# Raw left operands on GpSimd's DMA queue, a shorter pace for the last keys, fewer copies of x, and a last product in two banks

## The chip, the cores and the metric

The kernel runs on one core of a Trainium2 chip. The core has engines that run side by side, each through its own instructions in order: TensorE (PE, with its weight loads shown apart as PEld), VectorE (DVE), ScalarE (ACT), GpSimd (POOL) and SyncE (SP). DMAs are issued from the queues of SP, ACT and POOL and then run on 16 DMA engines. The metric is the device time of one execution in microseconds (us); lower is better. Three runs of the kernel before took 2245.58, 2249.1 and 2252.1 us (median 2249.1).

## What is computed

One inference step of a one-layer streaming encoder with two groups of eight heads: stick-breaking attention and retention. 1024 prompt rows and 8 x 16 sample rows (decoding against a cache of 1024 frames) go through it, all in fp32. Shortened:

```python
h = rms_norm(x, norm_pre)
q_sb, k_sb, v_sb, gate_sb, q_r, k_r, v_r, gate_r = split(h @ w_in)      # rope on q_r, k_r
o_sb = stick_breaking(q_sb, k_all, v_all)      # k_all: cached keys, then the new ones
o_r, state = retention(q_r, k_r, v_r, state)   # chunks of 64
y = concat(head_rms(o_sb) * g_sb * silu(gate_sb), head_rms(o_r) * g_r * silu(gate_r))
out = y @ w_out
x = x + rms_norm(out, norm_post)
```

The new keys, values and states are outputs too.

## The kernel before

**Products.** Each fp32 operand is split into a high part (ACT, L173) and the rest (DVE, L174), and a product is three passes on PE: high x high, high x low, low x high. The helper `split` does this for weights (raw tile `wr`, parts `wh`, `wl`) and for left operands (raw `mr`, `yr` or `ys`; parts `mh`, `ml` or `ah`, `al`). In the profile its work has lines L173 and L174 whatever calls it, so tiles tell who.

**Two stages.** The first stage projects and runs attention, in two groups of rows (0: prompt tiles 0 to 3 and the sample; 1: prompt tiles 4 to 7) and by heads, with projections on PE at L405 and L462. The second stage is the output product as a one-level Strassen scheme: seven products of half-size blocks, in two 512-column halves each, with PE at L1218, L1221 and L1222 (`times`). Their left operands are blocks of `s_y` (written by the heads) or sums of blocks (`s_s`, made by the `sums` jobs from `br`, L303 to L330); their weights are `w_out` or sums of its blocks (`s_b`), loaded at L1235 on SP's queue, two blocks ahead, into five buffers.

**The order of the work.** Side work is written as generators, here called jobs. While the program is recorded, `tick` is called after every few matmuls and moves each due job by a step; a `yield n` says how many ticks until the next step. A tick lies one and a half matmuls (in the first products of the second stage) to three matmuls apart. So the numbers in `yield` and in the D_ constants set where in each engine's order the work of a job stands. What an engine or a queue then waits for is decided by semaphores at run time. `pin` only ties a step to its place in the order and adds no wait of its own.

**The left operands.** `left` (L333) loads two rows of blocks at a time (a pair: 128 x 2 x 256 fp32, 256 KB) into `deep` buffers (three for `mr`, two for `yr`), yields `wait` ticks, and then splits one of eight blocks every D_OP = 2 ticks; after each second split it issues the load of the next pair that has no buffer yet. `left_sample` (L355) does the same with the sample's rows. Both issue on SP's queue (L343, L361), the queue of the weight loads. `both` (L1376) makes these jobs for the later products, with `wait` = D_LEFT // 3 = 8 ticks; the products of the middle of the first stage use D_LEFT = 24 and aren't touched.

**POOL's queue.** POOL issues the stick-breaking attention's transfers through memory (`s_be`, `be`, L653 and L662), the cached keys, `gpost` (the gain of the last norm, L1316) and the stores of the output that add to what is there (L1358). It also masks (L687).

**Decoding.** `decode` (L809) runs for each head beside the projections: keys come in eight loads, one step of the job each D_ZC = 23 ticks; then scores, weights, and the values `vc`, eight loads of 512 KB on SP's queue (L863) into six buffers, used by matmuls at L897 in an order of k = 0 to 7. The loads of k = 6 and 7 need the buffers of k = 0 and 1.

**Residuals.** `residuals` (L378) copies x to the output, one DMA of 512 columns by 128 rows at a time on ACT's queue, 36 in all, one every 50 ticks; later stores add to it or write over it.

**The end.** The last product (1, 1) is done in two halves of 256 columns in one PSUM bank. DVE subtracts each half from the row (L1484), ACT squares it with a sum (L1485), and the norm's small steps (L1489 to L1496) join both sums with `known`, that of the row's other parts.

Of the kernel before, what the change touches and what calls it, by code (L numbers as in the profile page):

```python
# [14 lines left out]
ALU = mybir.AluOpType  # L15
# [3 lines left out]
P = 128  # L19
D = 2048  # L20
KT = D // P
H = 8
# [15 lines left out]
D_ZP = (2, 2)  # L38
D_Z0 = (19, 11)
D_AV = (9, 11)  # L40
D_ZC = 23
D_ROW = 18
D_VC = (6, 36)
V_BUFS = 6
# [17 lines left out]
D_LEFT = 24  # L62
D_SUM2 = (4, 6, 26)
D_SUM3 = (3, 3, 6)
MR = 3
AHEAD = 2
HT = KT // 2
# [24 lines left out]
def tile_hybrid_step(  # L92
# [105 lines left out]
    def pin(*made):  # L198
        if anchor[0] is not None:
            for ins in made:  # L200
                tc.add_manual_dep(
                    ins.ins,
                    anchor[0].ins.name,
                    mybir.DependencyInfo(mybir.DependencyClass.NoSync, mybir.DependencyReason.SCHED_ONLY),
                    reason="not ahead of the products",
                )
# [126 lines left out]
    def left(gi, n, hi, lo, bufs, tag, deep, wait):  # L333
        src = LEFT[n]
        raw = []

        def load(pair):
            r = bufs.tile([P, 2, 256], F32, name=tag, tag=tag, bufs=deep)
            if src[0] == "y":
                rows = s_y[gi][src[1] * H // 2 + pair][:, :, src[2] * 256 : src[2] * 256 + 256]  # L340
            else:
                rows = s_s[gi][pair][:, :, src[1], :]
            pin(nc.sync.dma_start(r, rows))  # L343
            raw.extend((r[:, 0], r[:, 1]))

        for pair in range(deep):
            load(pair)
        yield wait
        for h in range(HT):
            pin(*split(hi[h], lo[h], raw.pop(0)))  # L350
            if h % 2 and h // 2 + deep < HT // 2:
                load(h // 2 + deep)
            yield D_OP

    def left_sample(kk, hi, lo, bufs, tag, deep, wait):  # L355
        raw = []
        for part in range(2):
            r = bufs.tile([P, HT // 2, P], F32, name=tag, tag=tag, bufs=deep)
            for i in range(2):
                pair = (kk * H + part * HT // 2) // 2 + i  # L360
                pin(nc.sync.dma_start(r[:, 2 * i : 2 * i + 2], s_y[0][pair][:, :, 4 * P : 5 * P]))  # L361
            raw.extend(r[:, i] for i in range(HT // 2))
        yield wait
        for h in range(HT):
            pin(*split(hi[h], lo[h], raw.pop(0)))
            yield D_OP

    preset = {}

    def after_preset(ins, t, c):  # L370
        tc.add_manual_dep(
            ins.ins,
            preset[t, c].ins.name,
            mybir.DependencyInfo(mybir.DependencyClass.Sync, mybir.DependencyReason.DATA),
            reason="the rows hold their input",
        )

    def residuals():  # L378
        for t in range(NT):
            for c in range(4):  # L380
                cs = slice(c * 512, (c + 1) * 512)
                preset[t, c] = nc.scalar.dma_start(y_rows(t)[:, cs], x_rows(t)[:, cs])
                pin(preset[t, c])
                yield 50

    def operand(pool, tags, n, **kw):
        made = [pool.tile([P, HT, n], F32R, name=t, tag=t, **kw) for t in tags]
# [88 lines left out]
    with ExitStack() as s1:  # L476
# [332 lines left out]
        def decode(h, qs, rest):  # L809
# [18 lines left out]
            for m in range(NB + 1):  # L828
                if m > 0 and m % 4 == 0:
                    s, ks = m // 4 - 1, ready[:4]  # L830
                    del ready[:4]
                    z = score_tile("zc")
                    for j in range(2):
                        for c in range(4):
                            r = slice(32 * c, 32 * c + 32)
                            mm = nc.tensor.matmul(  # L836
                                z[r, :],
                                qp[:, j, r],
                                ks[2 * j + c // 2][0][:, c % 2, :],
                                start=(j == 0),  # L840
                                stop=(j == 1),
                            )
                            if j == c == 0:

                                tc.add_manual_dep(
                                    mm.ins,
                                    ks[3][1].ins.name,
                                    mybir.DependencyInfo(
                                        mybir.DependencyClass.NoSync, mybir.DependencyReason.SCHED_ONLY
                                    ),  # L850
                                    reason="a set at a time",
                                )
                    with tc.issue_after(mm.ins):
                        with_scores()
                    sigmoids(kp, be, s * 512, z)
                if m + KC_AHEAD < NB:
                    load_k(m + KC_AHEAD)
                if m < NB:
                    yield D_ZC

            def load_v(k):
                vc = ip.tile([P, NB, P], F32, name="vc", tag="kv", bufs=V_BUFS)
# [443 lines left out]
    with ExitStack() as s3:  # L1306
# [68 lines left out]
        def both(n, groups):  # L1375
            made = []  # L1376
            for g in groups:
                mine[g, n] = operand(c3, ("ah", "al"), 256, bufs=2) if g else kept(at[n])
                made.append(left(g, n, *mine[g, n], *((rp, "yr", 2) if g else (wp, "mr", MR)), D_LEFT // 3))
            return made  # L1380

        def jobs_of(made):
# [33 lines left out]
        (first,) = both(1, G1)  # L1416
        more = Job(sums(fp, [sum_rows(1, h) for h in range(EARLY, H)], D_SUM3, 3), 30)
        Job(load_gpost(), 40)
        ready = [Job(left_sample(1, *mine["s", 1], fp, "ys", 2, D_LEFT // 3), 24)]
        for p in range(4):  # L1420
            outs[1, p] = rp.tile([P, D], F32, name=f"out{p}", tag=f"out{p}")
        Job(collect(1, 1, product(1, 1, G0, True, 2, first)), 1)
# [35 lines left out]
        for g, p in LAST:  # L1458
            key = g, 2 + p
            if g == 0:  # L1460
                load_row((1, p))
            a = bank()
            final = (g, p) == LAST[-1]
            halves = [slice(i * 256, i * 256 + 256) for i in range(2)]
            for hs in halves if final else (slice(0, 512),):
                for k in range(HT):
                    blocks = (half[k][:, hs] for half in keep)
                    times(a[:, hs], mine[g, 4], k, TS[p], *blocks, k == 0, k == HT - 1, k == 0)
                    if (g, p) == (0, 0):
                        tick()  # L1470
                        tick()
            if (g, p) == (0, 0):
                while jobs:
                    tick()
            o = area(key, 1)
            ssq = ssqs[key][0]
            known = rp.tile([P, 1], F32, name="known", tag="known", bufs=2)
            nc.vector.tensor_tensor(known, ssq[:, 2:3], ssq[:, 3:4], ALU.add)
            nc.vector.tensor_tensor(known, known, ssq[:, 0:1], ALU.add)
            nc.vector.tensor_scalar(known, known, 1.0 / D, EPS, ALU.mult, ALU.add)  # L1480
            base = [rp.tile([P, 1], F32, name=f"base{i}", tag=f"base{i}", bufs=2) for i in range(2)]
            sq = rp.tile([P, 512], F32, name="sq3", tag="sq3", bufs=1)
            for hs, part in zip(halves, base):
                nc.vector.tensor_tensor(o[:, hs], o[:, hs], a[:, hs], ALU.subtract)  # L1484
                nc.scalar.activation(sq[:, hs], o[:, hs], AF.Square, accum_out=part)  # L1485
            t = scaled[g][:, p, :]
            nc.vector.tensor_tensor(t, o, gpost[:, 512:1024], ALU.mult)
            v, hv, r, u = (rp.tile([P, 1], F32, name=f"end{i}", tag=f"end{i}") for i in range(4))
            nc.vector.tensor_scalar(v, base[0], 1.0 / D, known, ALU.mult, ALU.add)  # L1489
            nc.vector.tensor_scalar(v, base[1], 1.0 / D, v, ALU.mult, ALU.add)  # L1490
            nc.scalar.activation(r, v, AF.Sqrt)
            nc.vector.tensor_scalar(hv, v, -0.5, None, ALU.mult)
            nc.vector.reciprocal(r, r)
            nc.vector.tensor_scalar(u, r, r, hv, ALU.mult, ALU.mult)
            rs = rp.tile([P, 1], F32, name="rs", tag="rs", bufs=2)
            nc.vector.scalar_tensor_tensor(rs, u, 1.5, r, ALU.add, ALU.mult)  # L1496
            for c in (0, 2, 3, 1):
                part = t if c == 1 else area(key, c)
                x = rows[g, p][:, c * 512 : (c + 1) * 512]
                if c or final:  # L1500
                    for i, hs in enumerate(halves if final and c == 1 else (slice(0, 512),)):
                        nc.vector.scalar_tensor_tensor(part[:, hs], part[:, hs], rs, x[:, hs], ALU.mult, ALU.add)
                        store(key, c, (nc.sync, nc.scalar)[final and (c == 2 or i)], part[:, hs], hs)
                else:
                    nc.scalar.activation(part, part, AF.Copy, scale=rs)
                    add_out(key, c)
# [108 lines left out]
```

## Time and profile before

| | |
|---|---|
| median of three runs | 2249.1 us |
| the profiled execution, its own time | 2247.99 us |
| its span on the core | 2246.0 us |
| mean granted clock of TensorE | 0.997 |
| moved by DMA | 471.24 MB |

The span is what the profiler saw on the core; the profiled execution's own time has 2.0 us more around it. In the views, a row of a timeline has start and duration in us, engine, line, operation, output <- input, shape, and how many instructions it joins; the bracket at its end is the idle time just before it and what ended that. "SPq" and "ACTq" are a DMA's issue on that queue. A row of the waits has the engine and line that waited, what released it, and the total, the number and the longest of these waits. A row of the chain has start, duration and what the chain went through. A row of the DMA list ends with the size of each transfer and the median us from issue to landing. A row of windows has the length, then busy time and instructions of PE, PEld, DVE, ACT and POOL, the granted clock (1.00 is full), the share of DMA engines busy and GB/s.

### The profile page before, as it was taken

The page shows a single profiled execution, that of the slowest core. Times are in us where ns is not written, and L with a number is a line of the kernel's source. Part 1 is how long each engine was busy: PE and PEld are TensorE (multiplying, and loading weights), DVE is VectorE, ACT ScalarE, POOL GpSimd, SP SyncE. Part 2 cuts the span into 40 slices and gives each one's busy share as a digit, 9 for nine tenths or more (in the row PEclk, how much of TensorE's full clock was granted, in tenths as well). Part 3 has the DMA queues.
Part 4 walks back from the last instruction along what each step waited for, and adds up shares of the span by engine and source line. Part 5 has one row for each costly group of instructions (what it writes and reads, how often), then busy time and mean ns, then how long its engine had stood idle before and what let it go on. Part 6 is the DMA issues. An engine that isn't in the chain of part 4 may idle for free.

```text
span 2246.0 us, 34685 instructions
## 1 busy us (share of the span) xinstructions
PE 2217.6 (99%) x12026; PEld 1887.3 (84%) x12026; DVE 1266.2 (56%) x2690; ACT 919.8 (41%) x1999; POOL 432.2 (19%) x723
## 2 busy tenths in 40 slices
PE   8999999999999999999999999999999999999998
PEld 7888889798888979888788888888888888878887
DVE  5335445453444545356666675656666757646667
ACT  6423333333333333334333343443434445545563
POOL 1022131222213132221222111120202213000020
PEclk9999999999999999999999999999999999999999
DMA  8567575576657557678768778978888787765786
GB/s 290 172 200 202 175 195 172 179 194 209 185 180 192 183 170 198 204 202 278 223 183 237 231 230 239 242 229 232 232 242 231 219 230 199 234 204 165 223 205 181
DMA packets 383105, 471.24 MB, mean 210 GB/s; under 512 B 120400, under 2 KB 237904, under 8 KB 382416
## 3 DMA queue, kind: packets, MB, share of 16 engines
q1 hardware_dynamic: 252688, 290.84, 43.8%
q0 software_dynamic: 36432, 95.72, 15.6%
q10 hardware_dynamic: 93808, 82.46, 11.7%
q8 instruction: 94, 1.54, 0.3%
q14 instruction: 83, 0.68, 0.1%
HBM read 367.97 MB, written 110.36 MB: 213 GB/s over the span
## 4 chain that ended last, share of the span: by engine, by line
PE 87%; DMA 5%; DVE 3%; issue 3%; ACT 2%; SPq 1%; POOL 0%; DVEq 0%; ACTq 0%; POOLq 0%
PE accm L462 34%; PE acc L405 29%; PE a L1221 5%; PE a L1218 5%; PE a L1222 5%; PE z L768 2%; PE pa L795 2%; PE zc L836 1%; PE pd L897 1%; DMA s_rk<-rk 1%; DMA ro<-s_rk 1%; DMA wr<-w_cols 1%; DMA vc<-cache_v 1%; PE rs L918 1%; PE pa L936 1%
## 5 line engine op out<-in xcount | busy, mean ns | idle before, releaser
L173 ACT ACTIVATE wh<-wr 128x512 fp32r<-128x512 f32 x408 | 256.9, 631 | 481.8 <-PE acc L405 200.5
L462 PE MATMUL accm<-whn,mh 128*128 128x512 f32 x1152 | 452.6, 393 | 0.5 <-DVE rk L508 0.5
L462 PE MATMUL accm<-whn,ml 128*128 128x512 f32 x1152 | 452.6, 393 | 0.0
L462 PE MATMUL accm<-wln,mh 128*128 128x512 f32 x1152 | 452.1, 392 | 0.0
L405 PE MATMUL acc<-mh,wh 128*128 128x256 f32 (+2 forms) x1536 | 444.2, 340 | 7.3 <-ACT wh L173 7.3
L405 PE MATMUL acc<-ml,wh 128*128 128x256 f32 (+2 forms) x1536 | 446.4, 341 | 0.0
L405 PE MATMUL acc<-mh,wl 128*128 128x256 f32 (+2 forms) x1536 | 444.4, 340 | 0.0
L174 DVE TENSOR_TENSOR wl<-wr,wh 128x512 fp32r<-128x512 f32 x408 | 279.4, 688 | 268.8 <-ACT wh L173 253.6
L174 DVE TENSOR_TENSOR wln<-wrn,whn 128x512 fp32r<-128x512 f32 x256 | 175.5, 689 | 278.3 <-ACT whn L173 270.0
L173 ACT ACTIVATE whn<-wrn 128x512 fp32r<-128x512 f32 x256 | 161.2, 632 | 388.8 <-PE accm L462 268.4
L405 PEld LDWEIGHTS acc<-mh,wh 128*128 128x128 f32 x1536 | 284.1, 189 | 26.3 <-ACT wh L173 7.3
L405 PEld LDWEIGHTS acc<-mh,wl 128*128 128x128 f32 x1536 | 282.1, 189 | 23.9 <-issue 5.3
L405 PEld LDWEIGHTS acc<-ml,wh 128*128 128x128 f32 x1536 | 281.4, 189 | 19.3 <-issue 1.2
L462 PEld LDWEIGHTS accm<-whn,mh 128*128 128x128 f32 x1152 | 216.7, 188 | 44.7 <-DVE rk L508 1.3
L462 PEld LDWEIGHTS accm<-whn,ml 128*128 128x128 f32 x1152 | 216.7, 188 | 43.3 <-issue 0.8
L462 PEld LDWEIGHTS accm<-wln,mh 128*128 128x128 f32 x1152 | 216.6, 188 | 42.9
L662 POOL DMA_DIRECT2D be<-s_be x128 | 93.9, 739 | 150.1 <-DMA s_be<-be 127.0
L698 DVE TENSOR_TENSOR_SCAN kp<-kp 128x1152 f32<-128x1152 f32 (+4 forms) x40 | 82.6, 2066 | 55.3 <-POOL kp L693 28.0
L1218 PE MATMUL a<-wh,mh 128*128 128x512 f32 x240 | 94.8, 395 | 0.9 <-ACT mh L1278 0.9
L1222 PE MATMUL a<-wh,ml 128*128 128x512 f32 x240 | 93.7, 391 | 0.0
L1221 PE MATMUL a<-wl,mh 128*128 128x512 f32 x240 | 93.7, 390 | 0.0
L1218 PE MATMUL a<-wh,ah 128*128 128x512 f32 x208 | 82.4, 396 | 2.9 <-ACT wh L173 2.9
(285 smaller groups left out, 2942.5 us busy)
## 6 DMA issues: line engine op xcount, KB each, us to landing
wr<-w_cols SPq DMA_DIRECT2D x256, 256.0 KB, 4.5
wrn<-w_rows SPq DMA_DIRECT2D x256, 256.0 KB, 3.6
kcT<-cache_k POOLq DMA_DIRECT2D x64, 512.0 KB, 4.8
vc<-cache_v SPq DMA_DIRECT2D x64, 512.0 KB, 5.3
wr<-s_b SPq DMA_DIRECT2D x80, 256.0 KB, 3.9
wr<-w_out SPq DMA_DIRECT2D x80, 256.0 KB, 4.0
br<-w_out SPq DMA_DIRECT2D x64, 256.0 KB, 4.7
s_b<-br ACTq DMA_DIRECT2D x32, 512.0 KB, 5.5
```

What stands on the lines that cost most here:

```text
L173: nc.scalar.activation(hi, src, AF.Copy),
L174: nc.vector.tensor_tensor(lo, src, hi.bitcast(F32), ALU.subtract),
L405: last = nc.tensor.matmul(a[:, :m], lhs[:, j, :], rhs[w][:, j, o : o + m], start=(w == 0 and j == 0 and n == 0), stop=(w == KT // WQ - 1 a ...
L462: anchor[0] = nc.tensor.matmul(banks[t], lhs[q][:, j, ts], rhs, start=(k == 0 and n == 0), stop=(k == KT - 1 and n == 2),)
L662: q.dma_start(raw[32 * i : 32 * i + 32, :].rearrange("p (k a) -> p k a", a=32), s[:, :, 32 * i : 32 * i + 32].rearrange("k (j b) a -> b (k ...
L698: nc.vector.tensor_tensor_scan(rev, rev, rev, 1.0, ALU.mult, ALU.bypass)
L768: nc.tensor.matmul(z[:, :c], q2[a][:, i * P : (i + 1) * P], k2[b][:, s : s + c], start=(m == 0), stop=(m == 2),)
L795: nc.tensor.matmul(po[:, :P], at[:, j, :], rest["vn"][j], start=(j == 0), stop=(j == t))
L836: mm = nc.tensor.matmul(z[r, :], qp[:, j, r], ks[2 * j + c // 2][0][:, c % 2, :], start=(j == 0), stop=(j == 1),)
L1218: ins = nc.tensor.matmul(a, hi[k][:, ts], wh, start=first, stop=False)
L1221: nc.tensor.matmul(a, hi[k][:, ts], wl, start=False, stop=False)
L1222: anchor[0] = nc.tensor.matmul(a, lo[k][:, ts], wh, start=False, stop=last)
```

## The change

Five things are changed.

1. `left` and `left_sample` issue their loads on POOL's queue in place of SP's. 64 loads move.
2. The `wait` of the jobs that `both` makes, and of the second `left_sample`, is D_LEFT // 2 = 12 ticks in place of 8.
3. The last head's decoding (h = 7) paces its key steps by 20 ticks in place of 23.
4. `residuals` makes 23 copies in place of 36, one every 76 ticks: all four column blocks of tiles 0, 1, 4, 5 and of the sample, the first block of tiles 2, 3 and 6, none of tile 7. Stores to blocks without a copy no longer wait for one.
5. The two halves of the last product go to two PSUM banks, and each half's subtraction reads its own bank.

```diff
-D_ZC = 23
+D_ZC = 23, 20
...
-            pin(nc.sync.dma_start(r, rows))
+            pin(nc.gpsimd.dma_start(r, rows))
...
-                pin(nc.sync.dma_start(r[:, 2 * i : 2 * i + 2], s_y[0][pair][:, :, 4 * P : 5 * P]))
+                pin(nc.gpsimd.dma_start(r[:, 2 * i : 2 * i + 2], s_y[0][pair][:, :, 4 * P : 5 * P]))
...
+    PLAIN = 2, 3, 6, 7
...
+        if (t, c) not in preset:
+            return
...
+                if t in PLAIN and (c or t == PLAIN[-1]):
+                    continue
                 preset[t, c] = nc.scalar.dma_start(y_rows(t)[:, cs], x_rows(t)[:, cs])
                 pin(preset[t, c])
-                yield 50
+                yield 76
...
-                    yield D_ZC
+                    yield D_ZC[h == H - 1]
...
-                made.append(left(g, n, *mine[g, n], *((rp, "yr", 2) if g else (wp, "mr", MR)), D_LEFT // 3))
+                made.append(left(g, n, *mine[g, n], *((rp, "yr", 2) if g else (wp, "mr", MR)), D_LEFT // 2))
...
-        ready = [Job(left_sample(1, *mine["s", 1], fp, "ys", 2, D_LEFT // 3), 24)]
+        ready = [Job(left_sample(1, *mine["s", 1], fp, "ys", 2, D_LEFT // 2), 24)]
...
-            a = bank()
...
-            for hs in halves if final else (slice(0, 512),):
+            a = bank()
+            parts = [a[:, hs] for hs in halves]
+            if final:
+                parts[1] = bank()[:, halves[1]]
+            for hs, b in zip(halves, parts) if final else ((slice(0, 512), a),):
...
-                    times(a[:, hs], mine[g, 4], k, TS[p], *blocks, k == 0, k == HT - 1, k == 0)
+                    times(b, mine[g, 4], k, TS[p], *blocks, k == 0, k == HT - 1, k == 0)
...
-            for hs, part in zip(halves, base):
-                nc.vector.tensor_tensor(o[:, hs], o[:, hs], a[:, hs], ALU.subtract)
+            for hs, b, part in zip(halves, parts, base):
+                nc.vector.tensor_tensor(o[:, hs], o[:, hs], b, ALU.subtract)
```

What it does to the engines' orders is shown at three places. The changed program's lines are 5 higher from L387 to the last product and 8 higher behind it, and buffer numbers differ between the programs.

The first place is product 1 of group 1: during it, the left operands of group 0 for the next product, 2, are loaded (`mr` from `s_y0_4` to `s_y0_6`, blocks of the rows that the heads wrote). SP's queue of before, from the last pair of `yr`:

```order
L343 DMA yr_19471<-s_y1_3_141 128x2x256
L306 DMA br_19482<-s_y1_3_141 128x512
L306 DMA br_19482<-s_y1_7_145 128x512
L306 DMA br_19506<-s_y1_3_141 128x512
L306 DMA br_19506<-s_y1_7_145 128x512
L1235 DMA wr3_19599<-w_out 128x512
L1235 DMA wr3_19615<-w_out 128x512
L1235 DMA wr3_19634<-w_out 128x512
L1235 DMA wr3_19649<-w_out 128x512
L343 DMA mr_19576<-s_y0_4_134 128x2x256
L343 DMA mr_19578<-s_y0_5_135 128x2x256
L343 DMA mr_19580<-s_y0_6_136 128x2x256
```

POOL's queue of the change at the same place, with the sample's `ys` ahead:

```order
L343 DMA yr_19416<-s_y1_2_140 128x2x256
L361 DMA ys_19444<-s_y0_4_134 128x2x128
L361 DMA ys_19444<-s_y0_5_135 128x2x128
L361 DMA ys_19447<-s_y0_6_136 128x2x128
L361 DMA ys_19447<-s_y0_7_137 128x2x128
L343 DMA yr_19458<-s_y1_3_141 128x2x256
L1321 DMA gpost_19357<-norm_post 128x512 x2
L343 DMA mr_19559<-s_y0_4_134 128x2x256
L343 DMA mr_19561<-s_y0_5_135 128x2x256
L343 DMA mr_19563<-s_y0_6_136 128x2x256
L1321 DMA gpost_19357<-norm_post 128x512 x2
```

The three `mr` loads stood behind eight loads of sums and weights; now two `gpost` loads stand between them and `yr`.

The second place is the end of the last head's attention, which runs beside the second stage's product 5 of group 0; its left operands are the sums in `s_s`. SP's queue of before, around the fourth pair of `mr` from `s_s`:

```order
L1235 DMA wr3_18547<-s_b0_3_109 128x512
L1235 DMA wr3_18570<-s_b0_4_110 128x512
L343 DMA mr_18389<-s_s0_3_125 128x2x256
L1235 DMA wr3_18600<-s_b0_5_111 128x512
L662 DMA ro_18371<-s_rk1_7_18375 32x16x32 x4
```

POOL's queue of the change, from the first of these pairs:

```order
L343 DMA mr_18224<-s_s0_0_122 128x2x256
L343 DMA mr_18226<-s_s0_1_123 128x2x256
L343 DMA mr_18228<-s_s0_2_124 128x2x256
L692 AFFINE_SELECT kp_18269<-kp_18269 128x128
L692 AFFINE_SELECT be_18270<-be_18270 128x128
L658 DMA s_be7_4_18347<-be_18270 128x5x128
L667 DMA be_18270<-s_be7_4_18347 32x20x32 x2
L343 DMA mr_18377<-s_s0_3_125 128x2x256
L667 DMA be_18270<-s_be7_4_18347 32x20x32 x2
```

The fourth pair now stands behind the store of `s_be` and two of the four loads that read it back.

The third place is PE's order where the last head's decoding uses its values (L897 before, four rows for each k). Before:

```order
L889 MATMUL pd<-vv,kp 128x128
L897 MATMUL pd<-vc,kp 32x256 x24
L795 MATMUL pa<-vv,kb 128x128 x3
L405 MATMUL acc_11329<-mh_10322,wl 128x512
L405 MATMUL acc_11329<-mh_10407,wh 128x512
L405 MATMUL acc_11329<-ml_10408,wh 128x512
L405 MATMUL acc_11329<-mh_10407,wl 128x512
L897 MATMUL pd<-vc,kp 32x256 x4
L405 MATMUL acc_11329<-mh_10407,wh 128x512
L405 MATMUL acc_11329<-ml_10408,wh 128x512
L405 MATMUL acc_11329<-mh_10407,wl 128x512
```

Behind these comes one more matmul of L405 and then the four rows of k = 7. After the change, behind k = 0 to 3 (sixteen rows of L902) and nine matmuls of the projection (L410):

```order
L986 MATMUL pa<-st,rq 32x256 x4
L989 MATMUL pa<-vv,sc 128x128
L1020 MATMUL pSs_11224<-vv,rkn 128x128
L1020 MATMUL pSs_11225<-vv,rkn 128x128
L1020 MATMUL pSs_11224<-vv,rkn 128x128
L1020 MATMUL pSs_11225<-vv,rkn 128x128
L902 MATMUL pd<-vc,kp 32x256
L1020 MATMUL pSs_11236<-vv,rkn 128x128 x2
L1020 MATMUL pa<-vv,rkn 128x128 x2
L902 MATMUL pd<-vc,kp 32x256 x8
L800 MATMUL pa<-vv,kb 128x128 x2
L902 MATMUL pd<-vc,kp 32x256 x7
```

Between k = 3 and k = 6 the retention's matmuls (L986 to L1020) and the projection's now stand; before, k = 0 to 5 came in one piece.

At the very end, DVE's order before had both subtractions (L1484), the product with `gpost` (L1487), and then the two steps that add the halves' sums (L1489, L1490). Now the first of these steps stands between the two subtractions.

## The prediction

> **What bounds the kernel now.** I read the page first, then the waits of PE, then the windows and the chain around the two longest waits.
>
> ```profile
> span 2246.0 us, 34685 instructions
> PE 2217.6 (99%) x12026; PEld 1887.3 (84%) x12026; DVE 1266.2 (56%) x2690; ACT 919.8 (41%) x1999; POOL 432.2 (19%) x723
> PE 87%; DMA 5%; DVE 3%; issue 3%; ACT 2%; SPq 1%; POOL 0%; DVEq 0%; ACTq 0%; POOLq 0%
> ```
>
> PE is busy for 99% of the span and makes 87% of the chain that ended last, and the change removes no matmul. So it can only win back time in which PE stands still (2246.0 - 2217.6 = 28.4 us, the start and the end included) or runs at a lower clock. The waits of PE (in total, times, longest) say where it stands still:
>
> ```profile
> PE acc L405 <- ACT wh L173: 7.3, 1, 7.3
> PE a L1218 <- ACT wh L173: 2.9, 1, 2.9
> PE pd L897 <- DMA vc<-cache_v: 2.2, 2, 1.3
> PE rs L918 <- DVE rq L510: 1.9, 4, 1.3
> ```
>
> The 7.3 us are the kernel's start, which no edit touches. The 2.9 us and the 2.2 us lie where edits are. Windows over the first of them (the columns end in granted clock, DMA share and GB/s) show that it costs more than the wait:
>
> ```profile
> 1970.00:1978.60 8.60, 5.72 (x26) 4.38 (x24) 5.26 (x15) 2.72 (x8) 0.00 (x0) 0.98 0.87 295
> 1978.60:1985.20 6.60, 6.48 (x15) 4.78 (x16) 5.61 (x13) 3.70 (x9) 0.00 (x0) 0.51 0.68 223
> 1985.20:2000.00 14.80, 14.80 (x67) 12.23 (x66) 9.76 (x19) 10.94 (x24) 0.00 (x0) 1.00 0.80 269
> ```
>
> Behind the wait the clock is 0.51 for 6.6 us, in which 15 matmuls run where the next window fits one each 14.80/67 = 0.22 us. That is another 0.49 x 6.6 = 3.2 us: this one wait costs 2.9 + 3.2 = 6.1 us. POOL does nothing in all three windows.
>
> What releases it stands in the chain, in SP's queue and on ACT:
>
> ```profile
> 1971.78 5.84 DMA mr<-s_y
> ...
> 1963.11 0.56 SPq L343 DMA_DIRECT2D yr<-s_y  x1
> 1963.71 2.03 SPq L306 DMA_DIRECT2D br<-s_y  x4
> 1965.84 5.89 SPq L1235 DMA_DIRECT2D wr<-w_out  x4
> 1971.78 2.65 SPq L343 DMA_DIRECT2D mr<-s_y  x3
> ...
> 1977.65 0.42 ACT L173 ACTIVATE mh<-mr 128x256 fp32r<-128x256 f32 x1 [5.26 <-DMA mr<-s_y]
> 1977.97 1.13 ACT L173 ACTIVATE wh<-wr 128x512 fp32r<-128x512 f32 x2
> ```
>
> SP issues in order. Its four weight loads at 1965.84 take 5.89 us, since they wait for buffers; mr behind them is issued at 1971.78 and lands 5.84 us later. ACT stands before the split of mr from 1977.65 - 5.26 = 1972.39, and the weight splits that PE needs stand behind it.
>
> **The change, part by part.** *The raw left operands on POOL's queue, and the longer wait.* At this place POOL has nothing ahead of mr but loads that wait for nothing of the weights: the last yr, whose buffer a split frees at about 1963 (SP had it out at 1963.11), and two gpost loads. With 0.7 us for each issue (2.74 for four on POOL, below) the first mr leaves at about 1963.1 + 3 x 0.7 = 1965.2 instead of 1971.78. What POOL's queue takes to land is read from its other loads of that size:
>
> ```profile
> mr<-s_y SPq DMA_DIRECT2D x12, 256.0 KB, 5.4
> yr<-s_s SPq DMA_DIRECT2D x16, 256.0 KB, 4.0
> gpost<-norm_post POOLq DMA_DIRECT2D x4, 256.0 KB, 6.3
> out<-out POOLq DMA_DIRECT2D x9, 256.0 KB, 7.7
> out<-x_prompt ACTq DMA_DIRECT2D x32, 256.0 KB, 4.4
> ```
>
> With 6.3 us it lands at 1971.5, and with 7.7 at 1972.9. Twelve ticks instead of eight, at 1.5 matmuls (1.5 x 0.23 = 0.34 us; the chain's four L405 in 0.93, below) each, put ACT's split 1.4 us later, at about 1973.8. So ACT should find it there: **-6.1 us**. The bounds are 0 (mr still late) and -6.4 (with the first matmuls' slow starts behind the wait). What is late next is the same kind of split further on, which is the third rival.
>
> The same edit costs something earlier, where POOL still works for the last head's attention:
>
> ```profile
> 1858.45 0.53 SPq L343 DMA_DIRECT2D mr<-s_s  x1
> 1859.11 2.74 POOL L662 DMA_DIRECT2D be<-s_be  x4 [5.32 <-DMA s_be<-be]
> 1862.16 0.72 ACT L173 ACTIVATE mh<-mr 128x256 fp32r<-128x256 f32 x2 [1.22 <-DMA mr<-s_s]
> 1868.11 0.84 DVE L758 STREAM_TRANSPOSE kp<-be 128x640 f32<-128x640 f32 x1 [1.61 <-DMA be<-s_be]
> 1871.39 0.49 PE L918 MATMUL rs<-rq,rk 128*128 128x128 f32 x2 [1.29 <-DVE rq L510]
> ```
>
> The fourth mr load now stands behind two of the four be loads, which wait 5.32 us for s_be and start at 1859.11: it leaves at about 1859.11 + 2 x 0.69 = 1860.5, 2.0 us later, and lands 0.9 us slower than from SP (6.3 against 5.4), so ACT's split moves 2.9 us. DVE takes its work in order; of these 2.9 us its own wait of 1.61 at 1868.11 absorbs all but 1.3, and the rope behind it lets PE start at 1871.39 already 1.29 late. So PE waits about 2.6 us there, +1.3. Another +0.4 is for the loads behind the last head's be at 1890 to 1903, where PE waits for mh of L1278 today:
>
> ```profile
> PE a L1218 <- ACT mh L1278: 0.9, 2, 0.6
> ```
>
> Together **+1.7 us**, with 0 (POOL free in time) and +4.9 (1.7 + 3.2, half clock) as bounds. The loads that leave SP cost nothing there: SP's weight loads wait for buffers, as shown.
>
> A rule speaks against this edit: the Trainium skill, "DMA: Bandwidth & Descriptors", section "Specifications", gives about 1 us to the first byte from GpSimd's queue and 0.6 us from SP's or ACT's; by its figures each load would land 0.4 us later (an estimate from that page), and the sum here would not move, as mr lands before 1973.8 either way. The rows here say more than the Trainium skill does: 6.3 against 4.0 to 5.4 us is 0.9 to 2.3 us.
>
> *The last decode's shorter pace.* Where its values meet PE now:
>
> ```profile
> 1109.51 1.84 SPq L863 DMA_DIRECT2D vc<-cache_v  x2
> 1108.81 2.80 PE L897 MATMUL pd<-vc,kp 128*32 128x256 f32 x48
> 1114.65 0.64 PE L897 MATMUL pd<-vc,kp 128*32 128x256 f32 x8 [1.25 <-DMA vc<-cache_v]
> 1117.34 0.64 PE L897 MATMUL pd<-vc,kp 128*32 128x256 f32 x8 [0.93 <-DMA vc<-cache_v]
> ...
> 1107.73 0.93 PE acc L405 x4
> 1102.48 0.57 PE pa L981 x8
> 1103.05 0.42 PE pa L984 x2
> 1103.70 0.64 PE pSs L1015 x8
> ```
>
> Six value buffers hold k = 0 to 5; the loads of 6 and 7 go out once k = 0 and 1 are used, and land 1114.65 - 1108.81 = 5.8 and 8.5 us after the first matmul of k = 0. The pace alone moves this by 8 x 3 = 24 ticks and would shorten no wait. What does is that other matmuls of PE's order now stand between k = 3 and k = 6: four sets (32 x 0.058 = 1.9), nine projection matmuls (9 x 0.23 = 2.1), L981 and L984 (1.0), eight of L1015 (1.3), and two sets (0.9) come to 7.2 us before k = 6, so it doesn't wait; k = 7 follows a set and two L795 (0.7 us) later, at 7.9, and waits 0.6. PE waited 1.25 + 0.93 = 2.2 us: **-1.6 us**. Bounds: -2.2, and +0.5 if a weight load ahead of them in SP's queue holds them by 3 us. No key stands among PE's waits.
>
> *Copies of x.* Thirteen of the 32 counted transfers of 256 KB go from ACT's queue. They run on DMA engines while PE works, and the DMA share of the windows above, 0.68 to 0.87, leaves room; 23 x 76 ticks is as long as 36 x 50, so none ends later. With that cover gone one would cost at most its 4.4 us, once. I take **0**, with 1.5 us to either side for the neighbours that shift by an instruction or two from here on (PE's single waits are at most 1.3 us here).
>
> *Last halves in two banks.*
>
> ```profile
> 2235.36 0.75 DVE L1502 SCALAR_TENSOR_TENSOR ogsl<-ogsl,rs,x 128x512 f32<-128x512 f32 x1
> 2236.88 0.76 DVE L1484 TENSOR_TENSOR out<-out,a 128x256 f32<-128x256 f32 x2 [0.77 <-PE a L1222]
> 2238.27 0.21 DVE L1489 TENSOR_SCALAR end<-base,known 128x1 f32<-128x1 f32 x1
> 2237.39 0.42 ACT L1485 ACTIVATE sq<-out 128x256 f32<-128x256 f32 x1 [2.64 <-DVE out L1484]
> ```
>
> The first subtraction can run at 2236.1, when DVE is free, instead of 2236.88. But DVE's order now puts the L1489 step between the two subtractions, and that waits for ACT's square of the first half: 0.5 us after 2236.1 plus 0.4 and its 0.2 read, some 2237.4. The second subtraction then starts near 2237.5, not 2237.25, and L1490 follows 0.25 later: **+0.25 us** (-0.5 to +0.4).
>
> Sum: -6.1 + 1.7 - 1.6 + 0 + 0.25 = -5.75. The profiled execution took 2247.99 us (span 2246.0 and 2.0 around it), 1.1 under the median 2249.1 of the three runs: 2247.99 - 5.75 = **2242.2 us**, 0.31% under that median. About 0.3%, 6.75 us, is what a measurement of this kernel can tell from no change, so the forecast lies on the edge (2242.35) of that.
>
> **The rivals.** *Half clock moves to 1871.* The wait of 2.9 us at 1978 brought half clock, those of 1.3 us didn't; the new one of 2.6 lies between. If it does, 2242.2 + 3.2 = 2245.4 us, and with a microsecond or two of yr loads held behind others in POOL's queue up to 2248. For it: nothing but DVE's one wait covers. Against: 2.6 takes the full 2.9 us of delay. The Trainium skill, "TensorE: Matmul & The Clock Gate", Part 1, has the clock halved after an idle window of about 3.4 us; by that a gap of 2.6 us keeps full clock. Here 2.9 us sufficed, so the trace is stricter than that rule, and for 2.6 us no run shows it.
>
> *mr still comes late* (the change doesn't do what it says). PE starves if mr lands after 1977.62 - 2.91 = 1974.7, so if POOL issues it after 1974.7 - 6.3 = 1968.4. For it: it stands behind yr, which waits for a split. Against: 1968.4 - 1965.2 = 3.2 us to spare. The wait without half clock gives 2242.2 + 2.9 = 2245.1 us, the whole of it 2248.3.
>
> *Slower: late pairs in every later product.* With two buffers a yr pair is asked for after one split and needed six ticks on, at three matmuls (0.69 us) each 4.1 us later; two blocks of weights made ahead cover 2 x 6 x 0.23 = 2.8 us more. SP's 4.0 us fits; POOL's 6.3 fits inside 6.9; at 7.7 PE waits 0.8 each time, and from 4.1 + 2.8 + 2.9 = 9.8 us of landing each costs the 6.1 us above. Three such in the six products give 2242.2 + 18.3 = 2260.5. Against: only the accumulating stores reach 7.7.
>
> *Better.* The early cost of 1.7, the tail's 0.25 and k = 7's 0.6 don't come, and shifted neighbours give another 1: 2242.2 - 3.55 = 2238.7.
>
> **How the numbers follow.** Forecast (2239.8 to 2244.7) 0.56, better 0.14, half clock at 1871 0.17, mr late 0.08, slower 0.05. Of the forecast some 0.33 lies under 2242.35: faster 0.33 + 0.14 = 0.47, same 0.23 + 0.17 + 0.08 = 0.48, slower 0.05. The range 2236.5 to 2249.5 takes in the unknown copies on either side and the two rivals of no change; the slower case and the ends of the better one stay out, about 0.1.
>
> **What would show it.** Right: no wait of L1218 for wh near 1972 and clock 1.00 there; mr issued by POOL before 1968; one wait of about 0.6 at the last vc; about 2.6 at rs. Wrong: a window of clock 0.5 anywhere behind the start, PE waiting for ah or mh splits in the products on POOL loads of over 6.9 us, or a span that falls less than these waits do, which would put the copies' shift above my 1.5.

## The result, and the profile after

| | before | changed |
|---|---|---|
| median of six runs each | 2247.03 us | 2260.32 us |
| range | 2245.03 to 2252.10 | 2258.61 to 2261.32 |
| the profiled execution | 2247.99 us | 2259.97 us |
| its span | 2246.0 us | 2258.3 us |

The changed kernel is slower: its ratio to the kernel before is 1.0062, with a 95% interval of 1.0051 to 1.0073. That is 14 us more (13.3 between the medians), where 5.75 us less were forecast. Below, too, a difference in us is a ratio's distance from 1 times 2247 us.

The page and the waits of PE of the changed kernel:

```profile
span 2258.3 us, 34699 instructions
PE 2221.8 (98%) x12026; PEld 1890.4 (84%) x12026; DVE 1265.1 (56%) x2690; ACT 921.0 (41%) x1999; POOL 479.5 (21%) x787
...
PE rs L923 <- DVE rq L515: 4.7, 3, 4.3
PE pa L800 <- DVE kb L763: 4.5, 1, 4.5
PE a L1226 <- DVE wl L174: 4.1, 1, 4.1
PE a L1223 <- ACT mh L1283: 2.3, 2, 1.8
```

The two waits that the change was expected to end are gone: L1223 no longer waits for wh (2.9 us at L1218 before), and L902 no longer for vc (2.2 us at L897). Four others stand there instead. Windows from the start of PE's work behind each show what clock followed:

```profile
1123.70:1130.50 6.80, 6.78 (x23) 5.74 (x24) 3.52 (x13) 1.24 (x4) 4.89 (x8) 0.60 0.61 167
1879.60:1886.40 6.80, 6.77 (x30) 5.80 (x31) 3.67 (x9) 1.94 (x5) 3.40 (x6) 0.75 0.72 183
1923.90:1930.70 6.80, 6.77 (x23) 5.19 (x24) 2.12 (x4) 3.22 (x6) 0.00 (x0) 0.75 0.53 191
1988.40:1995.20 6.80, 6.75 (x22) 5.38 (x23) 6.80 (x18) 3.74 (x9) 0.14 (x1) 0.75 0.69 241
```

With (1 - clock) x 6.8 us added to each wait, and what the same place cost before taken off, the sum comes within 0.5 us of the difference of the two profiled executions:

| place | wait and slow clock, changed | before | difference |
|---|---|---|---|
| kb at 1123.7 (vc before) | 4.5 + 2.7 | 2.2 | +5.0 |
| rs at 1879.6 | 4.3 + 1.7 | 1.3 | +4.7 |
| L1223 at 1923.9 | 1.8 + 1.7 | 0.4 | +3.1 |
| wl at 1988.4 (wh before) | 4.1 + 1.7 | 2.9 + 3.2 | -0.3 |
| sum | | | +12.5, measured 2259.97 - 2247.99 = 12.0 |

**What the four wait for.** Each time an engine that works in order stands before a transfer that lands late. That it lands late because of what else is in flight is tested below for 1988 alone; at the other places it is argued. At 1988, two pieces of the chain, DVE's row, and the landing times of what was issued from 1973 to 1980 (the rows' last number is the median):

```profile
1975.72 10.15 DMA br<-s_y
1985.96 0.42 DVE br L325
...
1985.96 0.42 DVE L325 TENSOR_TENSOR br<-br 128x256 f32<-128x256 f32 x1 [7.25 <-DMA br<-s_y]
...
gpost<-norm_post POOLq DMA_DIRECT2D x4, 256.0 KB, 8.8
br<-s_y SPq DMA_DIRECT2D x4, 256.0 KB, 9.8
mr<-s_y POOLq DMA_DIRECT2D x3, 256.0 KB, 9.2
```

The kernel before issued from 1962 to 1975, at the same place:

```profile
wr<-w_out SPq DMA_DIRECT2D x5, 256.0 KB, 5.2
br<-s_y SPq DMA_DIRECT2D x4, 256.0 KB, 4.8
mr<-s_y SPq DMA_DIRECT2D x3, 256.0 KB, 5.8
```

POOL sent mr at 1975.05, even earlier than forecast (the first three rows of the table, 5.0 + 4.7 + 3.1 = 12.8 us, had moved this place, so 1965.2 became 1978.0). But it sent four gpost with them, and SP, now free of mr, its four br beside them: 11 transfers of 256 KB from 1973.9 on in place of one queue's work spread over ten us. The br loads land after 9.8 us in place of 4.8. DVE had stood before its first br in the kernel before too, which PE did not notice:

```profile
1969.10 0.42 DVE L325 TENSOR_TENSOR br<-br 128x256 f32<-128x256 f32 x1 [2.46 <-DMA br<-s_y]
```

Now it stands there for 7.25 us, and the weights' low parts that PE needs stand behind it.

At 1879 it is mr itself, on ACT:

```profile
1864.66 0.75 POOL L343 DMA_DIRECT2D mr<-s_s  x1
1872.11 0.72 ACT L173 ACTIVATE mh<-mr 128x256 fp32r<-128x256 f32 x2 [5.61 <-DMA mr<-s_s]
```

It takes 1872.1 - 1864.7 = 7.4 us, where SP's took 3.7. At 1923 it is weights on SP's queue, for which ACT stands twice:

```profile
1918.40 0.63 ACT L173 ACTIVATE wh<-wr 128x512 fp32r<-128x512 f32 x1 [2.77 <-DMA wr<-w_out]
1921.59 1.31 ACT L173 ACTIVATE wh<-wr 128x512 fp32r<-128x512 f32 x2 [2.56 <-DMA wr<-w_out]
```

The mh of L1283 stands behind these. No single edit is shown to make this wait: of the kernels below, `q_only` has none there, `r_only` one of 1.9 us, and `all_but_q`, which leaves out the copies too, none over 0.9. At 1123 it is the decode, with DVE's two rows, and the landing of the states' stores issued from 1101 to 1113, changed and before:

```profile
1118.60 0.06 DVE L681 MEMSET kp<- 128x1 f32 x1 [5.48 <-DMA out<-st]
1122.97 0.70 DVE L763 STREAM_TRANSPOSE kb<-kb 128x512 f32<-128x512 f32 x1
...
out<-st ACTq DMA_DIRECT2D x4, 128.0 KB, 8.4
...
out<-st ACTq DMA_DIRECT2D x4, 128.0 KB, 3.3
```

By the profile the fill of a new kp waits for the stores of the states, presumably for memory that it takes over from them. In the changed order it stands ahead of the kb transposition; before, it stood behind it. PE waits for kb from 1119.2 on.

### The profile page after: what moved, and what is told of

Its sections match the earlier page's. It is cut to its first block, busy times and chain, and to the rows that moved or that the text cites. A ratio compares the mean times of both kernels' runs of the same rounds, so it can differ in the third digit from the quotient of the medians.

```text
span 2258.3 us, 34699 instructions
## 1 busy us (share of the span) xinstructions
PE 2221.8 (98%) x12026; PEld 1890.4 (84%) x12026; DVE 1265.1 (56%) x2690; ACT 921.0 (41%) x1999; POOL 479.5 (21%) x787
## 5 line engine op out<-in xcount | busy, mean ns | idle before, releaser
L410 PE MATMUL acc<-mh,wh 128*128 128x256 f32 (+2 forms) x1536 | 444.0, 340 | 7.4 <-ACT wh L173 7.4
L410 PE MATMUL acc<-ml,wh 128*128 128x256 f32 (+2 forms) x1536 | 446.2, 341 | 0.0
L410 PE MATMUL acc<-mh,wl 128*128 128x256 f32 (+2 forms) x1536 | 445.3, 341 | 0.0
L410 PEld LDWEIGHTS acc<-mh,wh 128*128 128x128 f32 x1536 | 284.5, 189 | 26.8 <-ACT wh L173 7.4
L410 PEld LDWEIGHTS acc<-mh,wl 128*128 128x128 f32 x1536 | 282.7, 189 | 24.1 <-issue 5.3
L410 PEld LDWEIGHTS acc<-ml,wh 128*128 128x128 f32 x1536 | 281.8, 189 | 19.8 <-issue 1.2
L1223 PE MATMUL a<-wh,mh 128*128 128x512 f32 x240 | 95.8, 399 | 2.3 <-ACT mh L1283 2.3
L692 POOL TENSOR_SCALAR_AFFINE_SELECT kp<-kp 128x128 f32<-128x128 f32 x40 | 14.2, 355 | 382.7 <-ACT kp L686 382.7
```

The lines of the kernel that those rows point to most:

```text
L410: last = nc.tensor.matmul(a[:, :m], lhs[:, j, :], rhs[w][:, j, o : o + m], start=(w == 0 and j == 0 and n == 0), stop=(w == KT // WQ - 1 a ...
L692: nc.gpsimd.affine_select(blk, blk, pattern=[[-1, P]], base=0, channel_multiplier=1, compare_op=ALU.is_gt, fill=fill,)
L1223: ins = nc.tensor.matmul(a, hi[k][:, ts], wh, start=first, stop=False)
```

## The experiments

In all of them "before" was run beside the kernel on the same chip, so ratios are to that.

**The edits one at a time, or all but one.** `z_only` is the kernel before with the pace alone:

```diff
-D_ZC = 23
+D_ZC = 23, 20
...
-                    yield D_ZC
+                    yield D_ZC[h == H - 1]
```

> The kernel before with the shorter pace of the last keys alone. In its instruction order the last decode's pieces stand as in the changed kernel: on DVE the first fill of a new kp stands ahead of the transposition of kb that PE waits for. Theory A (pace): this edit alone moves the two 512 KB value loads, the kb loads and the stores out<-st into one time, out<-st lands in about 8 us instead of 3, DVE stands before the fill and PE waits about 4.5 us at L795 for kb, then half clock; the two vc waits of 2.2 us go: +5 us against before. Rival (copies or queue): the 4.5 us come from the other edits; alone the pace takes the vc waits away, as predicted: -1.6 us, no wait at L795 above 1 us.

Measured: 1.0024 (1.0015 to 1.0034), +5.4 us. Its waits and DVE's row:

```profile
PE pa L795 <- DVE kb L758: 4.4, 1, 4.4
...
1118.36 0.06 DVE L676 MEMSET kp<- 128x1 f32 x1 [5.66 <-DMA out<-st]
```

No wait for vc is left, as predicted, and the wait for kb comes from this edit alone.

`all_but_z` is the changed kernel with that edit undone.

> The changed kernel with the old pace (23 ticks for every head); the other four edits stay. Theory A (pace): the wait at L800 for kb goes, the vc waits of 2.2 us come back: 5 us under the changed kernel, about 7 us above before, with the waits at rs, at wh near 1912 and at wl near 1976 still there. Rival (the lag of 5 us from the first wait made the later ones): they go too, and it is within 3 us of before or under it.

Measured: 1.0031 (1.0019 to 1.0043), +7.0 us. The waits at vc are back (2.0 us), the one for kb is gone, and those at rs (4.6) and wl (3.7) stay: they don't come from the first one's delay.

`q_only` is the kernel before with the queue alone:

```diff
-            pin(nc.sync.dma_start(r, rows))
+            pin(nc.gpsimd.dma_start(r, rows))
...
-                pin(nc.sync.dma_start(r[:, 2 * i : 2 * i + 2], s_y[0][pair][:, :, 4 * P : 5 * P]))
+                pin(nc.gpsimd.dma_start(r[:, 2 * i : 2 * i + 2], s_y[0][pair][:, :, 4 * P : 5 * P]))
```

> The kernel before with the raw left operands on POOL's queue alone (wait of 8 ticks). Theory B (queue): mr of s_s lands in about 7 us instead of 3.7, PE waits about 4 us at rs, and POOL's burst of gpost and mr loads makes SP's br loads land in about 10 us instead of 5, so that DVE holds the weight splits near 1976 as long as mr did before: 5 to 8 us above before. Rival (queue harmless, the pace or the wait did it): the 2.9 us wait goes, no new one above 2 us: 4 to 6 us under before.

Measured: 1.0032 (1.0019 to 1.0046), +7.2 us.

```profile
PE rs L918 <- DVE rq L510: 6.1, 4, 5.5
PE a L1221 <- DVE wl L174: 4.2, 2, 4.0
...
1866.45 0.73 ACT L173 ACTIVATE mh<-mr 128x256 fp32r<-128x256 f32 x2 [6.70 <-DMA mr<-s_s]
```

Both waits come from the queue alone.

`all_but_q` is the changed kernel with the loads back on SP's queue.

> The changed kernel with the raw left operands back on SP's queue; wait of 12 ticks, pace, copies and banks as changed. Theory B: the waits at rs (4.3) and at L1223 near 1924 go back to 1.3 and 0.4; the kb wait of 4.5 stays; near 1978 the longer wait puts ACT's split 1.4 us later, so the 2.9 us wait shrinks to about 1.5 and keeps full clock: 8 to 10 us under the changed kernel, 0 to 3 us above before. Rival (queue harmless): the waits at rs and L1223 stay, at most 3 us under the changed kernel.

Measured: 1.0023 (1.0013 to 1.0032), +5.2 us, more than the 0 to 3 expected. The wait near 1978 shrank to 0.9 us with full clock, and in place of the 1.8 us one near 1924 none in that stretch is over 0.9. But rs still waits 2.3 us, which neither theory had: something else in this kernel costs some 3 us.

`w_only` is the kernel before with the longer wait alone, on SP's queue (twice, in `both` and for `left_sample`):

```diff
-D_LEFT // 3
+D_LEFT // 2
```

> The kernel before with the longer wait alone (12 ticks, loads on SP's queue). Prediction's step: ACT's split of mr stands 1.4 us later in the order, so the 2.9 us wait near 1978 shrinks by that to about 1.5, full clock stays, and the 3.2 us of half clock go: 3 to 5 us under before. Rival (SP's queue holds mr until after the split's place whatever the wait is, and other splits wait in its place): no less than 1 us under before, with a wait for wl or wh of over 2.5 us near 1978.

Measured: 0.9984 (0.9975 to 0.9994), -3.6 us, the fastest kernel of this study. The wait and the windows around it:

```profile
PE a L1221 <- DVE wl L174: 1.3, 1, 1.3
...
1980.00:1986.80 6.80, 5.53 (x25) 4.48 (x25) 5.96 (x14) 5.11 (x13) 0.00 (x0) 1.00 0.88 291
```

2.9 us became 1.3, and the clock stays full.

`r_only` has the thirteen copies left out and the pace of 76 ticks alone:

```diff
+                if t in PLAIN and (c or t == PLAIN[-1]):
+                    continue
                 preset[t, c] = nc.scalar.dma_start(y_rows(t)[:, cs], x_rows(t)[:, cs])
                 pin(preset[t, c])
-                yield 50
+                yield 76
```

> The kernel before with 23 copies of x, one every 76 ticks, alone. Prediction: nothing, within 1.5 us of before. Rival (the copies' new places collide with the loads and stores near the heads' ends, which would explain why all_but_q, without the queue, lies 5 us above before although the longer wait alone lies 3 us under it): 2 to 4 us above before, with waits of over 0.7 us at L800 or L923 that before does not have.

Measured: 1.0015 (1.0006 to 1.0024), +3.4 us. The prediction had nothing. The longest wait from 1870 to 1965 with `r_only`, and PE's busy time there before and with `r_only`:

```profile
PE a L1223 <- ACT mh L1283: 1.9, 1, 1.9
...
1870.00:1965.00 95.00, 92.74 (x444) 76.52 (x444) 62.12 (x125) 49.49 (x109) 16.07 (x22) 1.00 0.74 214
1870.00:1965.00 95.00, 90.49 (x425) 73.42 (x424) 61.06 (x120) 48.60 (x107) 15.02 (x23) 0.98 0.77 203
```

In the same 95 us 19 matmuls fewer are done, some 4 us of work at 92.74 / 444 = 0.21 us each: the busy time is 2.25 us shorter, and the wait of 1.9 us at 1918 brought half clock. This profiled execution was the slowest of its eleven (2255.19 against a median of 2249.99), and had a wait of 3.2 us at vc besides, so the trace isn't the median's. The waits at L800 or L923 that the rival named aren't there; those of the second stage are at L1223.

**Why the copies cost.** `tick` moves one due job and returns. A copy that is left out leaves its tick to another job, so steps of all the others move. `w_skip` has the longer wait and leaves the copies out, but their job still takes its 36 steps:

```diff
+                if t in PLAIN and (c or t == PLAIN[-1]):
+                    yield 50
+                    continue
...
-D_LEFT // 3
+D_LEFT // 2
```

> The longer wait (12), and the thirteen copies left out while their job still takes its 36 steps, one every 50 ticks; against before, PE's order then differs at 8 places where r_only's differs at 83. Theory (r_only lost its 3 us because a step that is left out gives its tick to another job and moves the other jobs' steps): as w_only, 2 to 4 us under before, and no wait of over 1 us at L800 or L1223 between 1870 and 1965. Rival (the copies' absence itself, or their later places, does it): within 1 us of before or above it, with such waits.

Measured: 0.9999 (0.9990 to 1.0008), the rival's time, not the 2 to 4 us less of the theory. The same stretch with `w_skip`, and then with `w_r_b` (below), which has the same longer wait and lets the steps move:

```profile
1870.00:1965.00 95.00, 92.92 (x446) 76.68 (x445) 63.55 (x125) 51.38 (x111) 16.91 (x23) 1.00 0.75 216
1870.00:1965.00 95.00, 90.20 (x430) 73.60 (x429) 59.56 (x119) 47.48 (x105) 14.15 (x22) 1.00 0.76 207
```

No copy is left to collide there (the last is issued at 1734.6 in `w_skip`, at 1713.0 in `w_r_b`, at 1716.3 in `r_only`), and no wait of `w_skip` in the second stage is longer than those of `w_only`. So the loss in this stretch does come from the moved steps. But `w_skip` isn't as fast as `w_only`: it has two waits of 1.6 us in the first stage, for kp at L801 (1437) and at L942 (1544), where the longest of `w_only` at these lines are 0.6 and 0.9. With one trace each this is not settled: the copies' absence may cost 2 to 3 us in the first stage by another way.

**What makes the transfers late.** `q_late` has the longer wait and POOL's queue for the later products alone:

```diff
-            pin(nc.sync.dma_start(r, rows))
+            pin((nc.gpsimd if wait < D_LEFT else nc.sync).dma_start(r, rows))
...
-D_LEFT // 3
+D_LEFT // 2
```

> The kernel before with the longer wait, and POOL's queue only for the loads of the later products and of the second sample operand; the first three loads of left operands (wait D_LEFT) stay on SP's queue. Theory B: the rs wait near 1871 is back at about 1.3 us, the one at wl near 1978 stays at about 4 us (br lands in about 10 us beside gpost and mr): 4 to 6 us under q_only, within 2 us of before. Rival (the rs wait comes from the longer queue of POOL in general): rs stays above 3 us.

Measured: 1.0012 (1.0003 to 1.0021), +2.7 us, and `q_late_gpost`, which moves gpost out of the way:

```diff
-        Job(load_gpost(), 40)
+        Job(load_gpost(), 120)
```

> q_late with the four gpost loads 80 ticks later, behind the yr loads of the next product. Theory (collision): without the megabyte of gpost beside them br and mr land in 5 to 7 us, the wait at wl near 1978 falls under 1.5 us and the clock stays full: 5 to 7 us under q_late, 4 to 6 us under before. Rival (br is late by its place in SP's queue behind weight loads): br still starts as late and the wait stays above 3 us.

Measured: 0.9997 (0.9987 to 1.0006), -0.7 us. The landing of what was issued around mr, `q_late` and then `q_late_gpost`:

```profile
gpost<-norm_post POOLq DMA_DIRECT2D x4, 256.0 KB, 9.3
br<-s_y SPq DMA_DIRECT2D x4, 256.0 KB, 10.3
mr<-s_y POOLq DMA_DIRECT2D x3, 256.0 KB, 9.8
...
br<-s_y SPq DMA_DIRECT2D x4, 256.0 KB, 7.5
mr<-s_y POOLq DMA_DIRECT2D x3, 256.0 KB, 6.7
```

rs is back at 1.2 us in `q_late`, while the wait for wl is 4.4: the two are separate costs of the queue. Without the megabyte of gpost beside them br and mr land 3 us earlier and the wait for wl falls to 2.1. That is the collision, but not all of it: br still takes 7.5 us, not 4.8, with mr still beside it, and another wait of 1.9 us for wh follows. It gained 3.4 us on `q_late` where 5 to 7 were expected, and is still 3 us behind `w_only`. POOL's queue buys nothing here. That mr beside it is what remains is argued; no run moved mr alone.

**What holds DVE in the decode.** `z_fill` is `z_only` with the fill of the large kp of group 1 on POOL:

```diff
-            nc.vector.memset(kp[:, n : n + 1], 1.0)
+            fill = nc.gpsimd if kind == "r" and phase[0] else nc.vector
+            fill.memset(kp[:, n : n + 1], 1.0)
```

> The shorter pace alone (z_only), but the fill of kp for the second group's large rows is done by POOL, which has nothing to do there, and no longer by DVE. Theory (an in-order engine held by the wait for out<-st): DVE goes on to the kb transposition, the 4.4 us wait at L795 falls under 1 us, half clock there goes, and the vc waits stay away: 5 to 7 us under z_only, 1 to 2 us under before. Rival (the kb loads themselves land too late): the wait at L795 stays at 3 us or more.

Measured: 1.0017 (1.0008 to 1.0027), +3.8 us. The theory of the fill alone falls:

```profile
PE pa L796 <- DVE kb L759: 3.5, 1, 3.5
...
1118.87 0.63 ACT L173 ACTIVATE kh<-kpast 128x512 fp32r<-128x512 f32 x1 [3.55 <-DMA out<-st]
1119.53 0.69 DVE L174 TENSOR_TENSOR kl<-kpast,kh 128x512 fp32r<-128x512 f32 x1 [3.50 <-ACT kh L173]
```

DVE passes the fill and stops a few instructions on, at the split of kpast. ACT makes its high part only at 1118.87, and by the profile that wait too ends with the stores of the states; kpast itself was issued at 1111.8 and took 6.6 us. What PE waits for is the kb transposition behind both, so it is the place of that transposition behind several waits for late transfers, not the one wait that was named.

**A still longer wait, and the copies and banks beside the wait.** `w_16` has 16 ticks (`D_LEFT * 2 // 3`) and nothing else.

> The kernel before with 16 ticks (D_LEFT * 2 // 3) in place of 8, loads on SP's queue, nothing else. Theory (ACT's place against mr's landing): 8 ticks left 2.9 us of wait and half clock, 12 left 1.3 and full clock, four more are 1.4 us, so no wait near 1978: 1 to 2 us under w_only, 4 to 6 us under before. Rival (the split's place is only moved and something else in the same order is late by then): a wait of 1 us or more for wl, wh or ah in the same product, no gain on w_only.

Measured: 0.9997 (0.9988 to 1.0006): the rival. Near 1980 the one wait has become several of 0.2 to 1.0 us. Its profiled execution was its slowest of eleven and had a wait of 3.6 us at vc, in a part of the program where its order is that of before.

`w_r_b` has the longer wait, the fewer copies and the two banks.

> Longer wait (12), fewer copies and two banks: the changed kernel without its two edits that were slower alone. If copies and banks cost nothing: 3 us under before, as w_only, with DVE's end 0.2 us later than before behind PE's last matmul. If the copies cost 2 to 4 us: at or above before.

Measured: 0.9995 (0.9986 to 1.0004), -1.1 us, between the two cases. In the second stage its trace has waits of 1.4 us for kp (L800) and 1.1 us for wh (L1223) that `w_only` doesn't have. From PE's last matmul's start to the end it takes 9.4 us, as before; the changed kernel itself 9.65.

## Why the prediction was wrong

1. *POOL's queue and the longer wait, -6.1 us.* Right on where mr is issued, and the wait of wh for it did end. The step that failed is "The loads that leave SP cost nothing there", together with taking 6.3 and 7.7 us as what POOL's queue takes to land. A landing time isn't a queue's property: at this place the same 256 KB took 4.8 to 5.8 us before, 9 to 10 with gpost and mr beside br, and 6.7 to 7.5 without gpost. The transfer that came too late for PE was br, one that the change doesn't touch and that the prediction didn't name. Net the place gained 0.3 us of 6.1.
2. *The same edit's early cost, +1.7 us.* Right in place and mechanism, too small by 3 us (+4.7 at rs): in `q_only` the issue moved by 2.0 us as worked out, but the load took 7.1 to 7.4 us in place of 3.7, not 0.9 us more, beside four ro, four be and a 512 KB store. The 0.9 set POOL's 6.3 us against 5.4, the median of other loads; this load's own rows had 3.7 (1858.45 to 1862.16). The wait of 4.3 to 5.5 us then brought slow clock, which the rival "half clock moves to 1871" had at a wait of 2.6. Of the +1.7, 0.4 were for mh behind the last head's be; that place cost 3.1 us more at 1923, but `q_only` has no wait there.
3. *The pace, -1.6 us.* Right that vc would no longer be waited for (0.6 was left in the forecast, none in the trace). What was missed is that 24 ticks move every other step of that decode too: the kb transposition fell behind a fill and a split that wait for transfers, and those land late: +5.4 us by `z_only`. In the changed kernel the last two value loads and five weight loads go out from 1102.3 to 1107.4, among the kb loads; before, SP sent these values only at 1109.5. That this makes the stores late is argued, not tested.
4. *The copies, 0.* +3.4 us by `r_only`. "None ends later" looked at the copies. The loss from 1870 to 1965 comes from the other jobs' steps, of which I let "an instruction or two" pass at 1.5 us. Whether that is the whole cost stays open, as `w_skip` keeps the steps and is still no faster than before.
5. *Two banks, +0.25 us.* 0.0 (`w_r_b`) to 0.25 (the changed kernel), by the tails above. The sum's own times add up to 2237.2, not 2237.4, for the end of L1489.
6. *The rivals.* The one that ends slower named 2260.5 us, but by late yr pairs in three later products; the trace has no such wait behind 2000. That the number is near is chance. Its point, late landing, was near the cause; the place was earlier in the program, and the late transfer not a yr pair.

Alone, the pace, the queue, the copies and the longer wait give 5.4 + 7.2 + 3.4 - 3.6 = 12.4 us against 14 measured together, with 2 to 3 us to either side for each.

## What to carry to other kernels

A load that is moved to an idle queue is issued earlier, and so meets transfers that it used to follow. List what will be in flight at the new time, on all queues, and ask which of these some in-order engine waits for (here one that did not move); take the landing time from the busiest stretch of the trace, not from a median. And where a change moves a job's steps, read the new order for what stands behind each wait, on every engine near the critical one: here a wait four ticks longer, which moved little, was worth more than the queue.

## What the runs showed of the hardware

- The granted clock fell to 0.50 behind much shorter waits than the 2.9 us of the kernel before. Over all traces of this study, the first wait of each kernel left out, no wait of PE of 1.73 us or less brought it, of the nine from 1.79 to 2.56 us seven did (the shortest 1.79, but not one of 2.14 and one of 2.56), and all of 2.9 us and more did. It lasted about 3.4 us in most of them and about 6.8 us in the others. The Trainium skill, "TensorE: Matmul & The Clock Gate", Part 1, speaks of about 3.4 us of idle time; the length of the slow stretch agrees with that figure, the wait that starts it doesn't.
- Landing times of equal loads at one place in the program went from 4.8 to 10.3 us with what else was in flight. The DMA share doesn't tell it: over 15 us at this place it was 0.86 in the kernel before (from 1963; br after 4.8 us) and 0.86 in `q_late` (from 1961; br after 10.3 us).
- With the same order of PE's instructions, the wait at vc was 1.1 and 1.0 us in one trace (`w_only`) and 3.6 us with half clock in another (`w_16`). A single trace places a cost; it doesn't size one of 3 us.
